# A hybrid attention and Hyena layer on one core: input loads placed further ahead of the casts that read them

## The chip, the cores and the metric

The kernel runs on one core of a Trainium2 chip. The metric is the device time of one execution in microseconds (us). PE is TensorE, DVE is VectorE, ACT is ScalarE, POOL is GpSimd, and SP is SyncE, which issues nearly all DMAs from one queue.

## The reference

One layer of an encoder over 2048 tokens of width 1024. One projection makes all inputs of two branches: windowed attention with a bias by relative position, and a long convolution (Hyena) whose filter is computed by a small network.

```
u = x @ w_in
q, k, v, a_gate, hy, h_gate, br_gate = split(u)
y_a = windowed_gqa(q, k, v, rel_bias, sink) * silu(a_gate)   # |i-j| <= 128, blocks of 128 queries
x0, x1, hv = split(short_conv(hy, conv_w, conv_b))           # width 3
h = sin(freq * (z @ w1 + b1)); h = sin(freq * (h @ w2 + b2)); h = sin(freq * (h @ w3 + b3))
h_f, h_b = decay * (h @ w4)                                  # the long filter, two sides
z = hv * x1
z = irfft(rfft(z) * rfft(filter)) + z * skip
y_h = z * x0 * silu(h_gate)
merged = g_a * (y_a @ w_branch_attn) + g_h * (y_h @ w_branch_hyena)
out = layer_norm(2 ** 0.25 * x + merged @ w_out)
```

There are 16 query heads and 4 heads of keys and values, each of width 64. All is fp32.

## The kernel before

**Numbers in two parts.** Each fp32 matmul operand is split into a high half (a cast to fp32r, `...h`) and a low half (the difference, `...l`), and a product is three matmuls: high by high, high by low, low by high. A split is thus a cast, mostly on ACT, and a subtraction on POOL or DVE, which waits for the cast. Names in the profile are those of tiles: `qh`, `ql`, `w4h`, `w4l`, `xq` (both halves of an input of a transform), `xS1h` and so on.

**Stages**, in order of the span: a projection stage for the first half of the channels (`hy_stage(0)`, to 375 us); the filter network (`filter_mlp`, L534) beside projections of keys, values and gates (to about 515); the filter's output, in units called quads (to 670); attention over the first eight heads (`attention(0)`, to about 1000, with projection work between its blocks); the second projection stage (1070 to 1380); the transform of the filter (to 1480); attention over the other heads (to 1850); 64 forward transforms of the convolution (`fwd`, L917, to 2150) with the attention branch's projection (`attn_out`, L1033) as filler; the inverse transforms; the merge and the output projection (2310 to the end).

**Order.** Each engine runs its instructions in an order that a scheduler decided when the kernel was built. The matmuls made with `mmo` keep the order of the program, and `tc.issue_after(x)` keeps what is under it behind `x`. So an instruction that waits holds back all that is behind it on its engine.

**Attention.** The work comes in groups: a pair of heads and two or three blocks of 128 queries. `groups` for the first half are of 3, 2 and 2 blocks, 24 groups with 56 blocks in all; for the second half they are of 3, with 72 blocks. At each step the loop (L826 to L846) issues the QK products of one block (`st_qk`, L720; PSUM `ps_a`), the transposes of the block before (`st_tr`; `ps_b`, then `ph` and `pl`) and the PV products of the one before that (`st_pv`; `ps_c`), with units of projection work between (`take`). `setup(i)` (L678) issues the loads of group i: bias, the q rows into `ql` (two buffers), the gate rows into `ag` (one buffer). `q_split(i)` (L700) casts `ql` to `qh` on ACT (L706) and subtracts on POOL in place (L707). It is placed behind the last exponential that the step issued:

```
                    if n == gctx[i]["b0"]:
                        setup(i + 1)
                    elif n == gctx[i]["b0"] + 1:
                        q_split(i + 1, last_exp[0])
```

`b0` and `b1` are the first and last block of group i, and n is the block of this step.

**Transforms.** `fwd_in(n)` (L907) loads the input of transform n, casts it on ACT (L911) and subtracts on POOL in two halves (L913). `x_half` gives it buffers, from a ring of 12 that the projection's operands used before. `enter_fft` calls it for the first `PRE` = 2 transforms at the end of attention 1, and `fft_next(n)` calls it for n + PRE after `fwd(n)`. `fwd` copies a product to `ka` on ACT (L927) and then runs six DVE operations (L931 to L936, and the split at L939). In the same time `load_big` (L115) brings `w_branch_attn` through the stage `ws` into the tiles `xA11`, `xA12`, `xS2` and `xS1`, with the subtraction on POOL.

**Filter.** `filter_mlp` computes the three sine layers in four parts of 512 columns: steps on DVE in tiles `sy` and `sk` (L553 to L561), the sine on ACT (L567). `filter_setup` (L584) then loads the last weights, `filt_w4`, in two parts into the ring of `sy` (L593 to L594) and splits them, the low half on DVE.

Of the kernel before, what the change touches and what calls it, by code (L numbers as in the profile page):

```python
# [8 lines left out]
F32 = mybir.dt.float32  # L9
# [5 lines left out]
P = 128  # L15
# [11 lines left out]
W_RING = 5  # L27
PRE = 2
LAST = (0.98, 0.99)
# [18 lines left out]
def hybrid_layer_kernel(ctx: ExitStack, tc: tile.TileContext, a: dict, out: bass.AP):  # L48
# [81 lines left out]
    with p1:  # L130
# [4 lines left out]
        zedge = const.tile([P, KT], F32, name="zedge")  # L135
        cw = const.tile([P, 24, 4], F32, name="cw")

        def consts():
            nc.sync.dma_start(out=cw, in_=a["conv"])
            nc.sync.dma_start(out=ident, in_=a["ident"])  # L140
            nc.sync.dma_start(out=sink, in_=a["attn_sink"].partition_broadcast(P))
# [201 lines left out]
        def hy_stage(p):  # L343
            base = 1024 * p
            with pool(f"hy{p}") as hy:
                hyp[0] = hy

                def raw(i):
# [107 lines left out]
                if p == 0:  # L456
# [10 lines left out]
                    for k in range(4):  # L467
                        r1.append(raw(4) if k % 2 == 0 else
                                  w_raw().rearrange("p a c -> p (a c)").rearrange("p (a c) -> p a c", a=2))
                        load_x(0, 1, k, r1[k])  # L470
                    consts()
                    for k in range(4):
# [61 lines left out]
        def filter_mlp(fl):  # L534
            Hv = h_d.rearrange("p a b -> p (a b)")
            fv = fl.tile([P, 4], F32, name="fv")
            nc.sync.dma_start(out=fv, in_=a["filt_vec"])
            w1 = fl.tile([66, P], F32, name="w1")
            w2 = fl.tile([P, P], F32, name="w2")
# [4 lines left out]
            for c in range(NCH):  # L544
# [3 lines left out]
                for l, w in enumerate((w1, w2, w3)):  # L548
# [14 lines left out]
                    if l < 2:  # L563
                        cur = fl.tile([P, CH], F32, name="sh", bufs=2)
                    else:
                        cur = fl.tile([P, CH], F32, name="H", bufs=2)
                    nc.scalar.activation(out=cur, in_=y, func=AF.Sin)  # L567
# [13 lines left out]
            for h in range(NH):  # L581
                nc.sync.dma_start(out=rep_d[h], in_=vec_d[h:h + 1].partition_broadcast(P))

        def filter_setup(fl, wr):  # L584
            dl = fl.tile([P, D], F32, name="dl")
# [5 lines left out]
            for g in range(2):  # L591
                gs = slice(g * CH, (g + 1) * CH)
                w4r = wr.tile([P, CH], F32, name="sy", bufs=2)  # L593
                nc.sync.dma_start(out=w4r, in_=a["filt_w4"][:, gs])  # L594
                split(w4h[:, gs], w4l[:, gs], w4r)
            s1k = fl.tile([P, 2, P], F32R, name="s1k")
# [46 lines left out]
        def attention(p, at, last=None):  # L643
# [34 lines left out]
            def setup(i):  # L678
# [6 lines left out]
                if g == 0:  # L685
                    if qt % 2 == 0:
                        load_kv(qt // 2)
                    for h in range(2):
                        bias[2 * qt + h] = at.tile([P, 384], F32, name="bias", bufs=3)
                        nc.sync.dma_start(out=bias[2 * qt + h], in_=skew(rep_d, 2 * qt + h))  # L690
                qh = at.tile([P, 2, 384], F32R, name="qh", bufs=2)
                ql = at.tile([P, 2, 384], F32R, name="ql", bufs=2)
                qv = q_d[qt, :, tok].rearrange("(h p) w -> p h w", h=2).bitcast(F32)
                for r in range(2):
                    nc.sync.dma_start(out=ql[r * 64:r * 64 + 64, :, 0:W].bitcast(F32), in_=qv)
                ag = at.tile([P, 384], F32, name="ag")
                nc.sync.dma_start(out=ag[:, 0:W], in_=ag_d[qt, :, tok])
                gctx[i] = dict(qt=qt, g=g, b0=b0, b1=b1, ag=ag, tok=tok, W=W, q=(qh, ql))

            def q_split(i, after=None):  # L700
# [122 lines left out]
            take(84 + 48)  # L823
            q_split(0)
            f0 = taken[0]
            for s in range(NS + 2):  # L826
                def part(x):
                    take(f0 + (total - f0) * min((s + PARTS[p][x]) / NS, 1.0))
                if s < NS:
                    st_qk(s)  # L830
                    i, n = steps[s]
                    if n == gctx[i]["b0"]:
                        setup(i + 1)
                    elif n == gctx[i]["b0"] + 1:
                        q_split(i + 1, last_exp[0])
                part(0)
                if s == NS and last:
# [13 lines left out]
        with pool("fc") as fc:  # L851
            with pool("ml") as ml:
                filter_mlp(ml)
                cs = filter_setup(fc, ml)
                run(stream([k_unit(ml, 0), v_unit(ml, 0)] + ag_units(ml, 0), mm))
# [50 lines left out]

        def fwd_in(n):  # L907
            f, g = divmod(n, 2)
            h, l = x_half(), x_half()
            last_ld[:] = [nc.sync.dma_start(out=l.bitcast(F32), in_=zk_d[:, f, g].bitcast(F32))]  # L910
            nc.scalar.copy(out=h, in_=l.bitcast(F32))  # L911
# [5 lines left out]
        def fwd(n, hl):  # L917
# [8 lines left out]
            k = fa.tile([P, CH], F32, name="ka", bufs=2)  # L926
            nc.scalar.copy(out=k, in_=kp)  # L927
            t1 = bank("t")
# [27 lines left out]
        wa, wg = [], []  # L956
        ins, ys = {}, {}

        def enter_fft(i):
            nonlocal fa  # L960
            if i == 0:
# [3 lines left out]
                for n in range(PRE):  # L965
                    fwd_in(n)
                wg[:] = [load_big("w_branch_attn", (nc.gpsimd, nc.gpsimd),
# [6 lines left out]
        def fft_next(n):  # L974
            f = n // 2
            if n + PRE < 64:
                fwd_in(n + PRE)
            if n % 2 and f + 1 < 32:
# [373 lines left out]
```

## Time and profile before

| what | us |
|---|---|
| median of three runs | 2743.44 |
| lowest and highest | 2738.68, 2751.53 |
| the profiled execution | 2745.46 |
| its span, from the first to the last instruction | 2743.7 |
| PE busy | 2547.3 (93%) |
| DVE, ACT, POOL busy | 1733.4, 1503.1, 1406.5 |

The profile is of one execution. Its mean granted clock of TensorE is 0.972 of full speed. Busy time of PE includes matmuls that run at the lower clock, so the time lost is found in two places: where PE is idle, and where the granted clock is below 1.00. A wait is put down to the instruction that ended it.

### The profile page before, as it was taken

The page shows a single profiled execution, that of the slowest core. Times are in us where ns is not written, and L with a number is a line of the kernel's source. Part 1 is how long each engine was busy: PE and PEld are TensorE (multiplying, and loading weights), DVE is VectorE, ACT ScalarE, POOL GpSimd, SP SyncE. Part 2 cuts the span into 40 slices and gives each one's busy share as a digit, 9 for nine tenths or more (in the row PEclk, how much of TensorE's full clock was granted, in tenths as well). Part 3 has the DMA queues.
Part 4 walks back from the last instruction along what each step waited for, and adds up shares of the span by engine and source line. Part 5 has one row for each costly group of instructions (what it writes and reads, how often), then busy time and mean ns, then how long its engine had stood idle before and what let it go on. Part 6 is the DMA issues. An engine that isn't in the chain of part 4 may idle for free.

```text
span 2743.7 us, 40487 instructions
## 1 busy us (share of the span) xinstructions
PE 2547.3 (93%) x13132; PEld 2143.8 (78%) x13132; DVE 1733.4 (63%) x3330; ACT 1503.1 (55%) x2897; POOL 1406.5 (51%) x1403
## 2 busy tenths in 40 slices
PE   6999999899998899999999999995999877999998
PEld 4888877686777777888877888884888766888887
DVE  8766677456666685665531777777899422555554
ACT  4444444477777674445555887886666443332231
POOL 6655545474656555655546666669666442211110
PEclk8999999999999999999999999998999998999999
DMA  5633443545444453346577444538787566644442
GB/s 199 213 123 115 133 134 124 164 154 203 124 124 132 132 173 121 100 129 201 176 242 237 133 137 141 154 111 283 236 256 236 201 217 216 204 154 154 150 139 81
DMA packets 275690, 456.54 MB, mean 166 GB/s; under 512 B 33513, under 2 KB 147515, under 8 KB 273925
## 3 DMA queue, kind: packets, MB, share of 16 engines
q1 hardware_dynamic: 273861, 444.90, 51.0%
q0 software_dynamic: 1616, 9.04, 1.0%
q8 instruction: 104, 1.70, 0.3%
q14 instruction: 109, 0.89, 0.1%
HBM read 294.42 MB, written 172.27 MB: 170 GB/s over the span
## 4 chain that ended last, share of the span: by engine, by line
PE 48%; DMA 9%; DVE 8%; POOL 3%; issue 3%; ACT 2%; SPq 0%; POOLq 0%; DVEq 0%; ACTq 0%
PE ps_y L53 8%; PE ps_a L53 4%; PE ps_c L53 4%; PE ps_y L271 4%; PE ps_y L273 4%; PE ps_y L275 4%; PE ps_zz L53 3%; PE ps_b L53 3%; PE ps_b L99 3%; DMA ga<-br_d 2%; DMA fl<-gc_d 2%; PE ps_zz L271 1%; PE ps_zz L275 1%; PE ps_zz L273 1%; DVE yl L57 1%
## 5 line engine op out<-in xcount | busy, mean ns | idle before, releaser
L57 POOL TENSOR_TENSOR w_l<-w_tmp,w_h 128x512 fp32r<-128x512 f32 x272 | 374.2, 1377 | 315.9 <-ACT w_h L56 277.7
L57 POOL TENSOR_TENSOR w_l<-w_raw,w_h 128x512 fp32r<-128x512 f32 x204 | 300.5, 1474 | 159.4 <-ACT w_h L56 131.5
L56 ACT CAST w_h<-w_tmp 128x512 fp32r<-128x512 f32 x272 | 168.2, 620 | 227.8 <-PE ps_y L273 174.1
L1157 POOL TENSOR_TENSOR ar<-ar,ga 128x256 f32<-128x256 f32 x64 | 48.3, 757 | 316.3 <-ACT ga L1156 177.1
L56 ACT CAST w_h<-w_raw 128x512 fp32r<-128x512 f32 x204 | 126.5, 621 | 152.3 <-PE ps_zz L273 88.6
L755 ACT ACTIVATE pb<-pb,rm 128x385 f32<-128x385 f32 (+1 forms) x256 | 153.2, 600 | 89.5 <-DVE rm L752 80.2
L913 POOL TENSOR_TENSOR xq<-xq 128x512 fp32r<-128x512 f32 x128 | 162.3, 1291 | 71.1 <-ACT xq L911 56.2
L370 DVE SCALAR_TENSOR_TENSOR cv<-u,cw,cv 128x1024 f32<-128x1024 f32 (+1 forms) x96 | 138.8, 1447 | 68.3 <-ACT cv L367 68.1
L271 PE MATMUL ps_y<-xq,w_h 128*128 128x512 f32 x376 | 152.1, 404 | 5.4 <-ACT u L283 5.2
L273 PE MATMUL ps_y<-xq,w_h 128*128 128x512 f32 x376 | 148.4, 395 | 0.0
L275 PE MATMUL ps_y<-xq,w_l 128*128 128x512 f32 x376 | 148.1, 394 | 0.0
L749 DVE CUSTOM_DVE_ANT_0 pb<-ps_a,bias 128x384 f32<-128x384 f32 (+1 forms) x256 | 130.1, 534 | 26.5 <-PE ps_a L53 22.5
L57 DVE TENSOR_TENSOR pl<-ps_b,ph 128x512 fp32r<-128x512 f32 (+1 forms) x240 | 128.5, 560 | 22.6 <-ACT ph L56 20.9
L224 DVE TENSOR_TENSOR w_tmp<-w_raw 128x512 f32<-128x512 f32 x94 | 97.1, 1033 | 57.8 <-DMA w_raw<-in_w_in_dram 40.3
L224 DVE TENSOR_TENSOR w_tmp<-w_raw,w_tmp 128x512 f32<-128x512 f32 x94 | 90.9, 967 | 63.5 <-POOL w_l L57 62.7
L283 ACT COPY u<-ps_y 128x512 f32<-128x512 f32 x204 | 118.8, 582 | 8.7 <-PE ps_y L275 8.0
L53 PE MATMUL ps_y<-xq,w_h 128*128 128x512 f32 x336 | 113.1, 406 | 1.2 <-ACT u L283 1.2
L56 ACT CAST ph<-ps_b 128x512 fp32r<-128x512 f32 (+1 forms) x240 | 106.7, 485 | 12.7 <-PE ps_b L99 10.5
L53 PE MATMUL ps_a<-k,ql 128*128 128x384 f32 (+1 forms) x256 | 86.7, 341 | 26.6 <-POOL ql L707 26.6
L287 DVE TENSOR_TENSOR ev<-ps_zz,u 128x512 f32<-128x512 f32 x72 | 49.4, 686 | 87.5 <-ACT u L283 41.2
L1000 PE MATMUL ps_y<-yh,b 128*128 128x256 f32 x344 | 99.7, 292 | 4.8 <-DVE ga L1158 4.7
L53 PE MATMUL ps_c<-pl,v 128*128 128x256 f32 x368 | 98.7, 294 | 5.5 <-DVE pl L57 5.1
(406 smaller groups left out, 8746.4 us busy)
## 6 DMA issues: line engine op xcount, KB each, us to landing
w_raw<-in_w_in_dram SPq DMA_DIRECT2D x136, 512.0 KB
xq<-zk_d SPq DMA_DIRECT2D x64, 512.0 KB
br_d<-ev SPq DMA_DIRECT2D x64, 256.0 KB
zk_d<-ko SPq DMA_DIRECT2D x64, 256.0 KB
zk_d<-zo SPq DMA_DIRECT2D x64, 256.0 KB
gc_d<-go SPq DMA_DIRECT2D x64, 256.0 KB
fl<-gc_d SPq DMA_DIRECT2D x32, 512.0 KB
ga<-br_d SPq DMA_DIRECT2D x64, 256.0 KB
```

The lines of the kernel that those rows point to most:

```text
L53: tc.keep_in_program_order(nc.tensor.matmul(*args, **kw))
L56: nc.scalar.copy(out=hi, in_=src)
L57: return (eng or nc.vector).tensor_tensor(out=lo, in0=src, in1=hi.bitcast(F32), op=ALU.subtract)
L224: w_sum[0].tensor_tensor(out=self.tmp[n], in0=i0, in1=i1, op=ALU.subtract)
L271: mmf(o, wh[:, k], xh[k], start=start and k == 0, stop=False, skip_group_check=not start)
L273: mmf(o, wh[:, k], xl[k], start=False, stop=False, skip_group_check=not start)
L275: mmf(o, wl[:, k], xh[k], start=False, stop=k == 3, skip_group_check=not start)
L283: nc.scalar.copy(out=u.tmp[n], in_=o)
L370: nc.vector.scalar_tensor_tensor(out=y[:, i0:hi], in0=u[:, i0 + n:hi + n], scalar=cw[:, t, n:n + 1], in1=y[:, i0:hi], op0=ALU.mult, op1=AL ...
L749: nc.vector.tensor_tensor_reduce(out=pb[:, 0:W], in0=sc[:, 0:W], in1=bias[head][:, off:off + W], scale=1.0, scalar=-3.0e38, op0=ALU.add, o ...
L755: last_exp[0] = nc.scalar.activation(out=pb[:, 0:W + 1], in_=pb[:, 0:W + 1], func=AF.Exp, bias=rm[:, 1:2], accum_out=rm[:, 2:3])
L913: nc.gpsimd.tensor_tensor(out=l[:, i], in0=l[:, i].bitcast(F32), in1=h[:, i].bitcast(F32), op=ALU.subtract)
```

## The change

Three places are changed, and one tile moves.

- In attention 0, the q rows of group i + 2 are loaded at the last block of group i (`q_load`), into a ring of three buffers, and `q_split(i + 1)` stands at the first block of group i, not the second. In attention 1 (p = 1) the split stays at the second block.
- In the transforms, a load and a split are now apart: the load is four transforms ahead (`PRE`), the split two ahead and behind the copy `ka` of the current transform.
- `filt_w4` is loaded into two tiles of its own ahead of the network's other weights, and its low half is subtracted on POOL. `H` has one buffer, not two.
- `cw`, the weights of the short convolution, is a tile of each projection stage, not of the whole program, and is loaded at the start of each.

```diff
-PRE = 2
+PRE = 4
...
-        cw = const.tile([P, 24, 4], F32, name="cw")
+        cw = None
...
             with pool(f"hy{p}") as hy:
                 hyp[0] = hy
+                cw = hy.tile([P, 24, 4], F32, name="cw")
+                if p == 1:
+                    nc.sync.dma_start(out=cw, in_=a["conv"])
...
             nc.sync.dma_start(out=fv, in_=a["filt_vec"])
+            w4 = []
+            for g in range(2):
+                w4.append(fl.tile([P, CH], F32, name="w4", bufs=2))
+                nc.sync.dma_start(out=w4[g], in_=a["filt_w4"][:, g * CH:(g + 1) * CH])
...
-                        cur = fl.tile([P, CH], F32, name="H", bufs=2)
+                        cur = fl.tile([P, CH], F32, name="H", bufs=1)
...
-                w4r = wr.tile([P, CH], F32, name="sy", bufs=2)
-                nc.sync.dma_start(out=w4r, in_=a["filt_w4"][:, gs])
-                split(w4h[:, gs], w4l[:, gs], w4r)
+                split(w4h[:, gs], w4l[:, gs], w4[g], nc.gpsimd)
...
+                if i not in qls:
+                    q_load(i)
                 qh = at.tile([P, 2, 384], F32R, name="qh", bufs=2)
-                ql = at.tile([P, 2, 384], F32R, name="ql", bufs=2)
-                qv = q_d[qt, :, tok].rearrange("(h p) w -> p h w", h=2).bitcast(F32)
-                for r in range(2):
-                    nc.sync.dma_start(out=ql[r * 64:r * 64 + 64, :, 0:W].bitcast(F32), in_=qv)
+                ql = qls.pop(i)
...
+            def q_load(i):
+                if i >= len(seq):
+                    return
+                qt, g = seq[i]
+                b0, b1 = groups[g]
+                W = (b1 - b0 + 1) * P
+                qls[i] = at.tile([P, 2, 384], F32R, name="ql", bufs=3 - p)
+                qv = q_d[qt, :, b0 * P:b0 * P + W].rearrange("(h p) w -> p h w", h=2).bitcast(F32)
+                for r in range(2):
+                    nc.sync.dma_start(out=qls[i][r * 64:r * 64 + 64, :, 0:W].bitcast(F32), in_=qv)
...
             q_split(0)
+            if p == 0:
+                q_load(1)
...
                         setup(i + 1)
-                    elif n == gctx[i]["b0"] + 1:
+                    if n == gctx[i]["b0"] + p:
                         q_split(i + 1, last_exp[0])
+                    if p == 0 and n == gctx[i]["b1"]:
+                        q_load(i + 2)
...
-        def fwd_in(n):
+        def fwd_load(n):
             f, g = divmod(n, 2)
-            h, l = x_half(), x_half()
-            last_ld[:] = [nc.sync.dma_start(out=l.bitcast(F32), in_=zk_d[:, f, g].bitcast(F32))]
+            raws[n] = x_half()
+            last_ld[:] = [nc.sync.dma_start(out=raws[n].bitcast(F32), in_=zk_d[:, f, g].bitcast(F32))]
+
+        def fwd_split(n):
+            l, h = raws.pop(n), x_half()
             nc.scalar.copy(out=h, in_=l.bitcast(F32))
...
-            nc.scalar.copy(out=k, in_=kp)
+            last_k[:] = [nc.scalar.copy(out=k, in_=kp)]
...
                 for n in range(PRE):
-                    fwd_in(n)
+                    fwd_load(n)
+                for n in range(2):
+                    fwd_split(n)
...
             if n + PRE < 64:
-                fwd_in(n + PRE)
+                fwd_load(n + PRE)
+            if n + 2 < 64:
+                with tc.issue_after(last_k[0].ins):
+                    fwd_split(n + 2)
```

The change shifts line numbers by up to some 30: the cast of q is L706 before and L725 after, its subtraction L707 and L726, the exponential L755 and L774; the subtraction of a transform's input is L913 and L938.

On ACT, in attention 0, at a group of two blocks, before the change (`L755` exponentials, `L763` the scaling of the second head, `ph` the cast of transposed probabilities, `w_h` filler):

```order
L763 ACTIVATE pb<-pb,rm 128x384
L755 ACTIVATE pb,rm<-pb,rm 128x385 x2
L56 CAST w_h<-w_tmp 128x512
L56 CAST ph_6454<-ps_b 128x512
L56 CAST ph_6461<-ps_b 128x256
L763 ACTIVATE pb<-pb,rm 128x384
L755 ACTIVATE pb,rm<-pb,rm 128x385 x2
L706 CAST qh<-ql 128x768
```

And after it, at the same place:

```order
L782 ACTIVATE pb<-pb,rm 128x384
L56 CAST w_h<-w_tmp 128x512
L774 ACTIVATE pb,rm<-pb,rm 128x385 x2
L725 CAST qh<-ql 128x768
L56 CAST ph_6456<-ps_b 128x512
L56 CAST ph_6463<-ps_b 128x256
L782 ACTIVATE pb<-pb,rm 128x384
L56 CAST w_h<-w_raw 128x512
L774 ACTIVATE pb,rm<-pb,rm 128x385 x2
```

The cast of the next group's q (128x768) stands behind the exponentials of the group's first block, and no longer behind those of its second.

On POOL, at the start of the transforms, before the change (`xS2l` and `xS1l` are low halves of `w_branch_attn`, `xq` those of transform inputs, two instructions for one input):

```order
L57 TENSOR_TENSOR xS2l<-ws,xS2h 128x512
L913 TENSOR_TENSOR xq<-xq 128x512 x4
L57 TENSOR_TENSOR xS1l<-ws,xS1h 128x512
L913 TENSOR_TENSOR xq<-xq 128x512 x2
L57 TENSOR_TENSOR xS1l<-ws,xS1h 128x512
L913 TENSOR_TENSOR xq<-xq 128x512 x2
L57 TENSOR_TENSOR xS1l<-ws,xS1h 128x512
L913 TENSOR_TENSOR xq<-xq 128x512 x2
L57 TENSOR_TENSOR xS1l<-ws,xS1h 128x512
L913 TENSOR_TENSOR xq<-xq 128x512 x20
```

And after it:

```order
L57 TENSOR_TENSOR xS2l<-ws,xS2h 128x512
L57 TENSOR_TENSOR xS1l<-ws,xS1h 128x512
L938 TENSOR_TENSOR xq<-xq 128x512 x2
L57 TENSOR_TENSOR xS1l<-ws,xS1h 128x512
L938 TENSOR_TENSOR xq<-xq 128x512 x2
L57 TENSOR_TENSOR xS1l<-ws,xS1h 128x512 x2
L938 TENSOR_TENSOR xq<-xq 128x512 x24
L57 TENSOR_TENSOR ayl<-ayl,ayh 128x512
```

Between the last `xS2l` and the last `xS1l` stand ten subtractions of transform inputs before the change and four after it. Counted from the start of the transforms, 36 stand ahead of the last `xS1l` before and 26 after.

On DVE, at the end of the filter network, before the change (`ev` ends a projection unit and frees its PSUM bank):

```order
L224 TENSOR_TENSOR w_tmp<-w_raw,w_tmp 128x512
L287 TENSOR_TENSOR ev<-ps_zz,u_4074 128x512
L57 TENSOR_TENSOR w4l<-sy,w4h 128x512
L224 TENSOR_TENSOR w_tmp<-w_raw 128x512
L57 TENSOR_TENSOR w4l<-sy,w4h 128x512
L287 TENSOR_TENSOR ev<-ps_y_4355,u_4343 128x512
L287 TENSOR_TENSOR ev<-ps_zz,u_4730 128x512
```

And after it:

```order
L223 TENSOR_TENSOR w_tmp<-w_raw,w_tmp 128x512
L286 TENSOR_TENSOR ev<-ps_zz,u_4074 128x512
L223 TENSOR_TENSOR w_tmp<-w_raw 128x512
L286 TENSOR_TENSOR ev<-ps_y_4355,u_4343 128x512
L286 TENSOR_TENSOR ev<-ps_zz,u_4730 128x512
```

The two subtractions `w4l` have left DVE, where they stood ahead of two `ev`; on POOL they stand near the start of the network.

## Rows read from the trace of the kernel before

**Rows 1.** Windows by stage: busy us of each engine, clock, DMA share, GB/s.

```profile
375.00:515.00 140.00, 127.87 (x542) 99.42 (x540) 96.57 (x141) 60.51 (x110) 64.06 (x46) 0.99 0.44 147
...
670.00:1045.00 375.00, 335.51 (x1751) 285.44 (x1751) 250.61 (x750) 256.97 (x595) 215.64 (x264) 0.95 0.47 145
...
1850.00:2150.00 300.00, 259.12 (x1463) 220.92 (x1462) 268.25 (x403) 194.62 (x320) 206.87 (x165) 0.95 0.74 243
```

**Rows 2.** Waits of PE, 670 to 1045: total us, times, longest.

```profile
PE ps_a L53 <- POOL ql L707: 25.1, 14, 3.9
PE ps_a L53 <- ACT qh L706: 5.1, 5, 3.1
```

**Rows 3.** Waits of PE in attention 1, 1475 to 1855.

```profile
PE ps_a L53 <- POOL ql L707: 1.4, 1, 1.4
```

**Rows 4.** Timeline of ACT, POOL and PE around one wait: start, duration.

```profile
756.69 0.60 ACT L755 ACTIVATE pb<-pb,rm 128x385 f32<-128x385 f32 x1
...
757.29 0.82 ACT L706 CAST qh<-ql 128x768 fp32r<-128x768 f32 x1
...
758.19 1.81 POOL L707 TENSOR_TENSOR ql<-ql,qh 128x768 fp32r<-128x768 f32 x1 [0.59 <-ACT qh L706]
...
760.05 0.39 PE L53 MATMUL ps_a<-k,ql 128*128 128x256 f32 x1 [1.29 <-POOL ql L707]
```

**Rows 5.** Windows of 20 us in attention 0.

```profile
700.00:720.00 20.00, 16.66 (x83) 14.28 (x82) 12.02 (x42) 11.69 (x28) 11.31 (x17) 0.83 0.35 103
...
940.00:960.00 20.00, 13.39 (x70) 11.32 (x69) 12.58 (x38) 12.98 (x30) 9.62 (x10) 0.83 0.39 130
...
980.00:1000.00 20.00, 16.82 (x81) 13.86 (x80) 19.30 (x38) 15.18 (x35) 14.34 (x14) 0.91 0.58 199
```

**Rows 6.** Windows: first to last QK of attention 0, and attention 1.

```profile
686.50:998.00 311.50, 274.40 (x1470) 235.60 (x1469) 217.55 (x694) 222.75 (x530) 186.30 (x242) 0.95 0.44 136
1497.00:1850.00 353.00, 347.08 (x1958) 304.14 (x1959) 270.85 (x895) 282.90 (x671) 234.51 (x301) 1.00 0.44 135
```

**Rows 7.** Timeline of SP's DMA issues in attention 0.

```profile
750.06 0.32 SPq L697 DMA_DIRECT2D ag<-ag_d  x1
...
756.08 1.24 SPq L695 DMA_DIRECT2D ql<-q_d  x2
```

**Rows 8.** Windows of 20 us in the transforms.

```profile
1870.00:1890.00 20.00, 12.29 (x42) 8.12 (x42) 19.33 (x30) 16.79 (x29) 20.00 (x17) 0.91 0.98 332
...
1910.00:1930.00 20.00, 10.29 (x47) 8.49 (x48) 10.19 (x16) 9.08 (x15) 16.11 (x14) 0.66 0.45 150
```

**Rows 9.** Waits of PE in the transforms, 1855 to 2155.

```profile
PE ps_b L53 <- POOL xS1l L57: 5.8, 2, 3.3
PE ps_b L53 <- ACT xS1h L56: 5.3, 2, 3.7
```

**Rows 10.** Groups of instructions, 1855 to 2155: count, busy us, mean ns.

```profile
L913 POOL TENSOR_TENSOR xq<-xq 128x512 fp32r<-128x512 f32 x122 | 154.6, 1291 | 68.3 <-ACT xq L911 56.2 <-PE ps_y L53 8.7 <-PE ps_c L53 1.9
```

**Rows 11.** Timelines of PE, DVE, ACT and SP at the filter network's end.

```profile
515.20 0.79 PE L271 MATMUL ps_y<-xA11h,w_h 128*128 128x512 f32 x1 [7.49 <-DVE ev L287]
...
519.06 0.40 PE L271 MATMUL ps_y<-xA11h,w_h 128*128 128x512 f32 x1
...
513.85 0.69 DVE L57 TENSOR_TENSOR w4l<-sy,w4h 128x512 fp32r<-128x512 f32 x1 [15.03 <-ACT w4h L56]
...
513.20 0.62 ACT L56 CAST w4h<-sy 128x512 fp32r<-128x512 f32 x1 [8.56 <-DMA sy<-in_filt_w_dram]
...
506.09 0.43 SPq L594 DMA_DIRECT2D sy<-in_filt_w_dram  x1
...
510.80 0.82 SPq L609 DMA_DIRECT2D hs<-h_d  x1
```

**Rows 12.** Matmuls that read `w4l`: ns min/median/max, first and last start.

```profile
L621 PE MATMUL ps_a<-w4l,hh x43: 387/393/398, 522.7 to 662.7; 128*128 128x512 f32 x43
```

**Rows 13.** A step of the network on DVE, in the same columns.

```profile
L559 DVE SCALAR_TENSOR_TENSOR sy<-sk,sy x36: 674/691/1791, 378.2 to 492.7; 128x512 f32<-128x512 f32 x36
```

More of the change, by code (lines that the diff above doesn't have):

```diff
@@ L135, in hybrid_layer_kernel @@
         zedge = const.tile([P, KT], F32, name="zedge")
-        cw = const.tile([P, 24, 4], F32, name="cw")
+        cw = None
         def consts():
-            nc.sync.dma_start(out=cw, in_=a["conv"])
             nc.sync.dma_start(out=ident, in_=a["ident"])
@@ L344, in hy_stage @@
             base = 1024 * p
+            nonlocal cw
             with pool(f"hy{p}") as hy:
                 hyp[0] = hy
+                cw = hy.tile([P, 24, 4], F32, name="cw")
+                if p == 1:
+                    nc.sync.dma_start(out=cw, in_=a["conv"])
                 def raw(i):
@@ L470, in hy_stage @@
                         load_x(0, 1, k, r1[k])
+                    nc.sync.dma_start(out=cw, in_=a["conv"])
                     consts()
@@ L582, in filter_mlp, with filter_setup @@
                 nc.sync.dma_start(out=rep_d[h], in_=vec_d[h:h + 1].partition_broadcast(P))
-        def filter_setup(fl, wr):
+            return w4
+        def filter_setup(fl, w4):
             dl = fl.tile([P, D], F32, name="dl")
@@ L698, in setup @@
                 gctx[i] = dict(qt=qt, g=g, b0=b0, b1=b1, ag=ag, tok=tok, W=W, q=(qh, ql))
+            qls = {}
+            def q_load(i):
[8 more added lines that the diff above has]
+                    nc.sync.dma_start(out=qls[i][r * 64:r * 64 + 64, :, 0:W].bitcast(F32), in_=qv)
             def q_split(i, after=None):
@@ L852, in hybrid_layer_kernel @@
             with pool("ml") as ml:
-                filter_mlp(ml)
-                cs = filter_setup(fc, ml)
+                cs = filter_setup(fc, filter_mlp(ml))
                 run(stream([k_unit(ml, 0), v_unit(ml, 0)] + ag_units(ml, 0), mm))
@@ L956, in hybrid_layer_kernel @@
         wa, wg = [], []
-        ins, ys = {}, {}
+        ins, ys, raws, last_k = {}, {}, {}, []
         def enter_fft(i):
```

## The prediction

> **What bounds the kernel now.** I read the windows by stage first. TensorE (PE) is busy 93% of the span, so time can only come out of its idle stretches and out of stretches at the lower clock. The first attention stage (670 to 1045) has 39.5 us without PE work and a mean granted clock of 0.95; the forward transforms (1850 to 2150) have 40.9 us and 0.95; the stretch of the filter network (375 to 515) has 12.1 us [rows 1]. The change touches these three.
>
> In the first, the waits of PE name one cause: `ps_a` (the QK product) waits 25.1 us in 14 places for POOL's q low half and 5.1 us in 5 places for ACT's q high half, together 30.2 us [rows 2]. In attention 1, which has the same functions, the first of these waits is 1.4 us, once [rows 3]. The timeline of one such wait shows why: ACT runs the second exponential of a block at 756.69, then the q cast at 757.29 (0.82 us), POOL subtracts at 758.19 for 1.81 us, and the next group's QK, already queued, starts at 760.05 after 1.29 us of waiting [rows 4]. The cast stands behind the exponentials of the group's second block, and in a group of two blocks the very next block belongs to the next group. Attention 1 has groups of three blocks and so one block more to spare.
>
> The waits cost the clock as well. Of the 20-us windows of this stage, four (from 700, 780, 900 and 940) show a granted clock of 0.83, a mixture of the two levels, 2.4 and 1.2 GHz; the first and the last of them stand in [rows 5]. The waits are in just those stretches.
>
> In the transforms DVE is the bound: busy 268.25 of 300 us [rows 1] and 19.33 of 20 us in a full window, but only 10.19 us in 1910 to 1930, where PE falls to 10.29 us and the clock to 0.66 [rows 8]. There `ps_b` waits 5.8 us for POOL's and 5.3 us for ACT's half of `xS1`, the last tiles of `w_branch_attn` [rows 9]. POOL, which had no idle time in the window at 1870 [rows 8], works in program order through subtractions for the transforms (122 of 1.29 us [rows 10]) and those of `xS1`.
>
> **Attention 0: the split one block earlier, the load one group earlier.** No instruction is added. Cast and subtraction move ahead by one block. A block of this stage takes 311.5 us / 56 = 5.6 us now [rows 6]. The longest wait for the low half is 3.9 us [rows 2], under one block, so in the usual case all are covered. I leave the 1.4 us that attention 1 still has: 30.2 − 1.4 = 28.8 us. For the clock, four windows lose 20 × 0.17 = 3.4 us each, 13.6 us at most; PE was idle in part of that time (3.34 of 20 us in the first, 6.61 in the last [rows 5]), and what fell into idle time cost nothing, so I take three quarters, 10 us. What is late next: ACT is busy 222.75 and DVE 217.55 of 311.5 us [rows 6]. If the stage shrinks to 273 us these are 82% and 80%; attention 1 runs at 80% and 77% (282.90 and 270.85 of 353) with clock 1.00 [rows 6], so the ordinary blocks can do it, but the end cannot shrink: in 980 to 1000 DVE is busy 19.30 us with x operands for the next stage [rows 5]. I give back 3 us. **Term: −36 us.** The ceiling comes from attention 1's rate: 353 us / 1958 matmuls = 0.180 us, times 1470 is 265 us, 46 us less than now [rows 6]. The floor is three quarters of the waits and nothing of the clock, −22 us.
>
> The load has to be there for the earlier cast. SP issues in order, and in the row of interest it sits on the gate load `ag` until 750.06 and then on the q load, which waits for the QK that reads its buffer, until 756.08 [rows 7]. With a third buffer that second wait is gone, and the new place of the q load is right behind that `ag` load, some 6 us sooner, against a cast some 5.6 us sooner. So the lead stays what it is, and it is enough now.
>
> **Transforms: loads four ahead, splits two ahead.** The casts, subtractions and loads are as many as before. ACT, which sat on late inputs, gets them earlier. By the order, 26 subtractions of transform inputs stand ahead of the last `xS1` subtraction where 36 did: 10 × 1.29 = 12.9 us of POOL less [rows 10]. But the new splits wait for the current transform's copy `ka`, so POOL will idle for perhaps half of that. I let 6 of the 11.1 us of waiting [rows 9] go, and 1 us for the half clock there. **Term: −7 us**; the ceiling is both waits, −11 us, since DVE at 19.33 of 20 us leaves nothing elsewhere. Against it: two more input loads before the first transform. The window at 1870 moves 332 GB/s at a DMA share of 0.98 [rows 8], so 2 × 0.5 MB delay the matrices and weights behind them by up to 3.2 us; the bound is +3 us.
>
> **Filter network.** The second `filt_w4` load is issued at 506.09, behind the stores of `rep_d`; ACT waits 8.56 us for it until 513.20; DVE's subtraction follows at 513.85; the `ev` of a finished unit is queued behind that on DVE, and its PSUM bank holds PE for 7.49 us until 515.20. The nine matmul starts from there to 519.06 are 0.43 us apart, the pace of the lower level [rows 11]; at the upper one they would take half, 1.9 us less. With `w4` loaded 130 us earlier, 7.5 + 1.9 = 9.4 us come free. Late next is `hs`, issued at 510.80 [rows 11]: the first matmul of the filter's output stood at 522.7 [rows 12] and would come to 513.3, where `hs` has hardly landed and still needs a cast. I give back 2.9 us for that and a clock that dips anyway. **Term: −6.5 us**, bounds −2 and −9.4.
>
> POOL's two subtractions of `w4` come near 380, off any wait. Some DVE steps of the network's chain take up to 1791 ns there, against a median of 691 [rows 13], so by that row two more overlaps cost 2 × 1.1 = 2.2 us. The chain is hidden behind projection matmuls until its end; if `hs` is what is late next, the term is −4.3. The Trainium skill, SBUF — State Buffer, section "Who interferes with whom", speaks against moving work to POOL: a DVE instruction with two SBUF inputs and a GpSimd one that reads SBUF exclude each other, and whoever issues first keeps the other out for its whole length. By that rule the same two steps would wait up to 1.3 us each; the trace agrees in kind, with the 1791 ns.
>
> **The rest.** `w4` first means two issues of 0.43 us [rows 11] ahead of the network's small weights: 0 to 0.9 us, taken as 0, because projections fill PE then. The convolution weights are loaded a second time before the second projection stage, one small load where SP has room: 0, bound 7 us (from the issue at 506.09 to the landing at 513.20, a queued load [rows 11]).
>
> **Sum.** −36 − 7 − 6.5 = −49.5 us. The profiled execution took 2745.46 us around a span of 2743.7; it becomes 2696. That execution is 2.0 us above the median of 2743.44, so the median becomes **2694 us**. The three runs before lie 0.47% apart; 0.5%, 13.7 us, is about what can be told from no change.
>
> **Rivals.** (1) *Only part of the waits returns, because ACT takes the cast ahead of the softmax of the second block.* The cast of 0.82 us [rows 4] now stands before that block's reads of `ph` and its exponentials, and ACT at 82% has little slack; then `ps_c` waits where `ps_a` did. For it: the chain of one block runs through ACT several times. Against it: attention 1 carries the cast between blocks as well, and waits little. Attention −22, transforms −3, filter −4: −29, giving 2714 us.
>
> (2) *The change does not do what it says in attention 0*, because q loads come late: SP is stuck on `ag` [rows 7] beyond the cast and ACT stops for the landing. Only the other two terms, −13.5, are left: 2730 us. Against it: the lead worked out above.
>
> (3) *Slower, in the transforms.* The split of input n+2 is issued after the copy `ka` of transform n, together with `ayl` subtractions on the same engine. If POOL's half comes after the PE wants it by one subtraction (1.29 us [rows 10]) in each of 62 transforms, that is +80 us against −42.5 elsewhere: 2781 us. It turns the sign from 0.7 us each on. Against it: POOL is busy 206.87 of 300 us [rows 1], and a transform lasts over 4 us, so the low half has about two of them.
>
> (4) *More*: all waits [rows 2, 9, 11] and the clock: −46 − 11 − 9 = −66, 2677 us.
>
> **Chances.** The forecast (2682 to 2706) 0.62; rival 1 0.22; rival 2 0.06; rival 3 0.04; rival 4 0.06. The range 2672 to 2722 holds the forecast, rival 4 and most of rival 1. Faster by over 0.5%: forecast, rivals 1 and 4 and half of rival 2, 0.93; within 0.5%: the other half, 0.03, and a small rival 3, 0.01; slower 0.03.
>
> **What would show it.** In the profile after: the wait of `ps_a` for `ql` and `qh` in attention 0 under 5 us, that stage's clock near 1.00 and its length near 336 us; ACT's wait for `w4h` gone and PE's 7.49 us down to 2 or less; PE's waits for `xS1` below 6 us. Rival 1 shows as `ps_c` waiting for `ph` or `pl`, rival 2 as ACT's cast waiting for a DMA, rival 3 as PE's `ps_a` waiting for `xq` from POOL in the transforms. What would make it wrong most: a new wait in attention 0 that keeps the clock at 0.83, since the clock and the waits of this stage are three quarters of the sum.

## The result and the profile after

The changed kernel takes 2703.25 us (median of 4, 2699.46 to 2711.21) against 2747.49 of the kernel before on the same chip: ratio 0.9835, 95% interval 0.9811 to 0.986, so 1.65% faster. The profiled execution took 2705.55 us, with a span of 2703.8 and a mean clock of 0.977. The forecast was 2694, range 2672 to 2722.

The total is near, but one of the three terms went the other way. I compare the two traces by the first and last start of what begins and ends a stage (us, from the start of the span; QK is the product of queries and keys, the first matmuls of an attention block):

| stretch | before | after | difference |
|---|---|---|---|
| start to the first QK of attention 0 | 686.5 | 697.9 | +11.4 |
| first to last QK of attention 0 | 311.7 | 277.9 | −33.8 |
| from there to the first QK of attention 1 | 497.5 | 501.1 | +3.6 |
| first to last QK of attention 1 | 354.1 | 349.5 | −4.6 |
| last QK to the last forward transform | 289.1 | 282.5 | −6.6 |
| from there to the end of the span | 604.8 | 594.9 | −9.9 |

**Attention 0** did what was forecast. These are the windows from the first to the last QK of both stages, in the columns of [rows 6]:

```profile
697.90:975.80 277.90, 265.10 (x1471) 230.38 (x1470) 213.46 (x690) 219.64 (x525) 187.13 (x242) 0.98 0.49 151
1477.00:1826.00 349.00, 343.82 (x1954) 302.10 (x1955) 267.99 (x894) 282.70 (x671) 232.66 (x298) 1.00 0.45 137
```

Beside [rows 6], PE's idle time in attention 0 went from 37.1 us (311.50 − 274.40) to 12.8 (277.90 − 265.10), 24.3 less, and the busy time of the same 1470 matmuls from 274.4 to 265.1, 9.3 less, since fewer of them run at the lower clock (0.95 to 0.98). The list of PE's waits, 690 to 1010, names no `ql` and no `qh` any more; what is late next is small (the first of these two waits was 2.0 us before):

```profile
PE ps_c L53 <- DVE pl L57: 6.6, 11, 1.2
PE ps_c L53 <- ACT pb L774: 5.0, 1, 5.0
```

The lower clock is left at the stage's end alone. The 20-us windows have 1.00 up to 920, then 0.83, 0.91 and 0.91; the first of the slow ones, which holds the wait of 5.0 us for `pb`, is

```profile
920.00:940.00 20.00, 14.95 (x70) 12.57 (x69) 13.47 (x36) 13.34 (x32) 12.10 (x14) 0.83 0.43 139
```

**Transforms.** PE's waits from 1826 to 2126, to be read beside [rows 9]:

```profile
PE ps_a L53 <- POOL xq L938: 8.3, 5, 4.5
...
PE ps_c L53 <- DMA mat<-s_d: 5.0, 1, 5.0
...
PE ps_b L53 <- POOL xS1l L57: 1.8, 1, 1.8
```

The waits for `xS1` fell from 11.1 us to 1.8. In their place stand 8.3 us for inputs that POOL has not yet subtracted. The 5.0 us for the first matrix only look new: the kernel before waits nearly as long at the same matmul, the first of the transforms, where the wait is put down to DVE's `ya`. The timelines of PE show it, first before, then after:

```profile
1861.76 1.62 PE L53 MATMUL ps_c<-xq,mat 128*128 128x512 f32 x3 [4.59 <-DVE ya L812]
```

```profile
1837.15 1.62 PE L53 MATMUL ps_c<-xq,mat 128*128 128x512 f32 x3 [5.01 <-DMA mat<-s_d]
```

It starts 12.0 us behind the last QK before and 10.8 us after.

**Filter.** The stretch that [rows 1] shows with 12.1 us of idle PE has 8.8 now, but its clock fell from 0.99 to 0.96, and the quads behind it have 9.1 us idle, against 3.1 (155.00 − 151.94) in the same window before:

```profile
375.00:515.00 140.00, 131.24 (x534) 100.90 (x533) 104.00 (x141) 60.11 (x110) 59.85 (x46) 0.96 0.40 132
515.00:670.00 155.00, 145.91 (x592) 112.08 (x592) 98.27 (x129) 105.46 (x185) 91.41 (x77) 0.97 0.44 152
```

The wait of 7.49 us [rows 11] is gone. In its place, in the timelines of ACT and PE, stand an early one for `filt_w4` and a late one for the network's output:

```profile
370.36 0.62 ACT L56 CAST w4h<-w 128x512 fp32r<-128x512 f32 x1 [3.80 <-DMA w<-in_filt_w_dram]
...
524.08 0.80 PE L627 MATMUL ps_a<-w4h,hh 128*128 128x512 f32 x1 [3.64 <-ACT hh L56]
```

### The profile page after: what moved, and what is told of

Its sections match the earlier page's. It is cut to its first block, busy times and chain, and to the rows that moved or that the text cites. A ratio compares the mean times of both kernels' runs of the same rounds, so it can differ in the third digit from the quotient of the medians.

```text
span 2703.8 us, 40522 instructions
## 1 busy us (share of the span) xinstructions
PE 2535.4 (94%) x13132; PEld 2136.0 (79%) x13132; DVE 1738.7 (64%) x3328; ACT 1500.6 (56%) x2897; POOL 1414.5 (52%) x1405
## 4 chain that ended last, share of the span: by engine, by line
PE 63%; DVE 13%; DMA 13%; issue 4%; ACT 4%; POOL 3%; SPq 1%; DVEq 0%; POOLq 0%; ACTq 0%
PE ps_y L53 9%; PE ps_y L270 7%; PE ps_y L272 6%; PE ps_y L274 6%; PE ps_a L53 4%; PE ps_c L53 4%; PE ps_zz L53 3%; PE ps_b L99 3%; PE ps_b L53 3%; DMA ga<-br_d 3%; PE ps_zz L270 3%; PE ps_zz L272 3%; PE ps_zz L274 3%; DMA fl<-gc_d 2%; DVE yl L57 1%
## 5 line engine op out<-in xcount | busy, mean ns | idle before, releaser
L938 POOL TENSOR_TENSOR xq<-xq 128x512 fp32r<-128x512 f32 x128 | 162.6, 1295 | 60.5 <-ACT xq L936 58.9
L774 ACT ACTIVATE pb<-pb,rm 128x385 f32<-128x385 f32 (+1 forms) x256 | 153.2, 600 | 72.2 <-DVE rm L771 61.5
L57 DVE TENSOR_TENSOR pl<-ps_b,ph 128x512 fp32r<-128x512 f32 (+1 forms) x240 | 130.1, 560 | 12.8 <-ACT ph L56 11.2
L99 PE MATMUL ps_b<-ident,pb 128*128 128x128 f32 x736 | 102.6, 275 | 0.0
```

The costliest lines, as they stand in the source:

```text
L57: return (eng or nc.vector).tensor_tensor(out=lo, in0=src, in1=hi.bitcast(F32), op=ALU.subtract)
L99: return nc.tensor.transpose(out=o, in_=i, identity=ident)
L774: last_exp[0] = nc.scalar.activation(out=pb[:, 0:W + 1], in_=pb[:, 0:W + 1], func=AF.Exp, bias=rm[:, 1:2], accum_out=rm[:, 2:3])
L938: nc.gpsimd.tensor_tensor(out=l[:, i], in0=l[:, i].bitcast(F32), in1=h[:, i].bitcast(F32), op=ALU.subtract)
```

## The experiments

Twelve kernels ran, four at a time on one chip, each four beside runs of the kernel before (medians 2746.01, 2751.88 and 2750.38 us). So ratios to the kernel before are compared, not times; the bracket behind a ratio is its 95% interval. The first four take the change apart.

**e1_no_filter**: the changed kernel without its filter part.

```diff
-            w4 = []
-            for g in range(2):
-                w4.append(fl.tile([P, CH], F32, name="w4", bufs=2))
-                nc.sync.dma_start(out=w4[g], in_=a["filt_w4"][:, g * CH:(g + 1) * CH])
...
-                split(w4h[:, gs], w4l[:, gs], w4[g], nc.gpsimd)
+                w4r = wr.tile([P, CH], F32, name="sy", bufs=2)
+                nc.sync.dma_start(out=w4r, in_=a["filt_w4"][:, gs])
+                split(w4h[:, gs], w4l[:, gs], w4r)
```

> The changed kernel without its filter part: filt_w4 comes through the ring of sy at the end again and is split on DVE. Theory A (the filter part costs time: in the profile after, the first QK of attention 0 starts 11.4 us later than before): about 2703 - 11 = 2692 us, and the first QK back at about 686 us. Theory B (as predicted, the filter part gains 6.5 us, and the late start has another cause, such as the conv weights' tile or a difference between executions): about 2703 + 6.5 = 2710 us, and the first QK stays near 698 us.

Measured: 0.9822 (0.979 to 0.9854), 2694.51 us; the first QK at 687.7. Theory A by the trace; the ratio alone does not part it from the whole change.

**e2_q_only**, **e3_fft_only** and **e4_filter_only**: the kernel before with the lines of one part of the diff each (with the first, `cw` moves too).

```diff
-                    elif n == gctx[i]["b0"] + 1:
+                    if n == gctx[i]["b0"] + p:
```

> The kernel before with the attention part alone (q split a block earlier, q load a group earlier, three buffers, and the conv weights in the projection stages, which make the room). Theory A (the stage's 33.8 us from the first to the last QK are this part's): 34 us less than before, about 2713 us, with the first to the last QK of attention 0 in 278 us. Theory B (a third or more of the stage's gain comes from what the filter part puts ahead of it, work that now runs before the first QK): no more than 23 us less, about 2724 us, with that stretch at 288 us or more.

Measured: 0.9854 (0.9833 to 0.9874), −40 us of 2746; first to last QK 274.1 us. Theory A.

```diff
-PRE = 2
+PRE = 4
...
+                with tc.issue_after(last_k[0].ins):
+                    fwd_split(n + 2)
```

> The kernel before with the transforms' part alone. Theory A (6.6 us, as between the two profiles from the last QK to the last transform): about 2740 us. Theory B (the inverse and merge stages, 9 us shorter in the profile after, owe this to the transforms' part too): 15 us less, about 2732 us. Theory C (nothing, what xS1 gives is lost to the matrix load and the POOL waits): 2747 us.

Measured: 0.9958 (0.9943 to 0.9972), −12 us; last QK to last transform 284.7 us. Between A and B: the stage itself gave 4.4 us, and the rest is not in one place.

```diff
-                split(w4h[:, gs], w4l[:, gs], w4r)
+                split(w4h[:, gs], w4l[:, gs], w4[g], nc.gpsimd)
```

> The kernel before with the filter part alone. Theory A: 11 us more than before, about 2758 us, slower by 0.4%, with the end of the network's chain some 8 us later. Theory B: 6.5 us less, about 2741 us.

Measured: 1.0044 (1.0028 to 1.006), +12 us. Theory A: the filter part alone makes the kernel slower. The chain of the network ended at 503.0 us, against 494.7 before.

The next two divide the filter part.

**e5_filter_late**: loads behind the first features, split behind the last sine.

```diff
-                split(w4h[:, gs], w4l[:, gs], w4[g], nc.gpsimd)
+                with tc.issue_after(last_sin[0].ins):
+                    split(w4h[:, gs], w4l[:, gs], w4[g], nc.gpsimd)
```

> The changed kernel with filt_w4 still in tiles of its own, but loaded behind the network's small weights and first features, and cast and subtracted behind the network's last sine. Theory A (the filter part loses by its early cast: ACT waits 3.8 us for the load at 370 us with the work of a projection unit behind it, and the network's chain slides 8.6 us; the order of the quads costs the rest): the chain ends near 497 us, the first quad comes at 515 to 519, the first QK at about 691 instead of 698 us, in all about 2696 us. Theory B (the early cast is harmless, the whole loss is the order in which the quads are run): first QK at 697 us, 2703 us.

Measured: 0.9861 (0.9837 to 0.9884); chain's end 503.3, first QK 705.3. Theory A fell: without the early cast the chain was as late, and PE waited 5.3 us more, for an `ev` on ACT just ahead of the first QK. Nor is it B alone, since the chain still ended late.

**e6_own_tiles_only**: as e1, but `filt_w4` in tiles of its own (and `H` with one buffer).

```diff
-                w4r = wr.tile([P, CH], F32, name="sy", bufs=2)
+                w4r = wr.tile([P, CH], F32, name="w4", bufs=2)
```

> The changed kernel without its filter part, except that filt_w4 has tiles of its own instead of the ring (and H one buffer): loads and splits stand in the program where they stood before, behind the stores of the bias rows. The order of the quads on PE then is that of the changed kernel. Theory A (the order of the quads at their end costs 6 to 9 us by itself): from the first quad to the first QK 170 us or more, against 163 us without the filter part; first QK at 694 us or later, about 2700 us. Theory B (the order of the quads costs nothing): 163 us for that stretch, first QK at 688 us or earlier, about 2693 us.

Measured: 0.9807 (0.9784 to 0.983). Without the ring to wait for, SP issued the loads at 371.93 although they stand late in the program, and ACT waited 6.3 us for the first of them, but the chain ended at 496.9 and the first quad came at 517.5, 7.1 us sooner than in e1. From there to the first QK it took 173.5 us against 163.1. Theory A by that stretch, though the first QK, at 691.0, came sooner than it said (694).

Two divide the attention part.

**e7_q_split_only** and **e8_q_load_only**, both from e2:

```diff
-            if p == 0:
-                q_load(1)
...
-                    if p == 0 and n == gctx[i]["b1"]:
-                        q_load(i + 2)
```

> Attention part alone, with the cast a block earlier and three buffers, but the load issued by setup, one group ahead as before. Theory A (the earlier load is needed): ACT's cast waits for its DMA in most groups, 1 us or more each; the stretch from the first to the last QK is 285 us or more instead of 274, in all about 2716 us. Theory B (a third buffer lets SP issue the load early enough from its old place): 274 us and 2704 us, as with the whole attention part.

Measured: 0.9834 (0.9812 to 0.9856); first to last QK 274.8 us. Theory B: with a third buffer the old place of the load does as well.

```diff
-                    if n == gctx[i]["b0"] + p:
+                    if n == gctx[i]["b0"] + 1:
```

> Attention part alone, with the load two groups ahead into three buffers, but the cast at its old place in the group's second block. Theory A (the place of the cast is the cause): PE still waits some 30 us for q, the stretch stays at 311 us, about 2746 us. Theory B (the loads were late): 275 us and 2706 us.

Measured: 1.0001 (0.9982 to 1.0019); 311.6 us. Theory A. PE's waits, 680 to 1010, stay those of [rows 2]:

```profile
PE ps_a L53 <- POOL ql L723: 26.1, 14, 4.3
PE ps_a L53 <- ACT qh L722: 5.6, 6, 3.2
```

**e9_h_ring**: the whole change with another filter part. `filt_w4` goes into the two buffers of `H`, loaded ahead of the stores of `rep_d`, split on DVE.

```diff
+            for g in range(2):
+                w4.append(fl.tile([P, CH], F32, name="H", bufs=2))
+                nc.sync.dma_start(out=w4[g], in_=a["filt_w4"][:, g * CH:(g + 1) * CH])
             nc.sync.dma_start(out=vec_d, in_=vec)
```

> The changed kernel with another filter part: filt_w4 goes into the two buffers of H, loaded in the program ahead of the stores of the bias rows (SP then issues the second load behind 8 of the 16 stores), split on DVE. The quads keep the order of the kernel before. Theory A (the loss is the sliding chain plus the order of the quads, and the wait for filt_w4 was worth 7 us): chain's end near 497 us, first quad at 517 to 520, first QK at 681 to 684 us, in all 2687 to 2690 us, better than without the filter part (2694). Theory B (hs and the rest of SP's queue hold the first quad anyway): first quad at 523 us or later, first QK at 687 us, 2694 us.

Measured: 0.9809 (0.9788 to 0.9831), 2695.52 us; first quad 519.2, first QK 683.6. Theory A by the trace, though the total is 5 us above what it said. Its interval overlaps those of the change, of e1 and of e6, so the ratio does not make it the best of them.

**e10_filter_dve**: the whole change, the low half of `filt_w4` on DVE.

```diff
-                split(w4h[:, gs], w4l[:, gs], w4[g], nc.gpsimd)
+                split(w4h[:, gs], w4l[:, gs], w4[g])
```

> The changed kernel with the low half of filt_w4 subtracted on DVE, as before the change, loads and tiles as in the change. Theory A (POOL's two subtractions at 371 us hold a weight's low half, DVE waits 3.1 us for it and the chain slides): the chain ends near 497 us, first QK at 691 us, about 2697 us. Theory B (where it is subtracted does not matter; the load ahead of the small weights, ACT's wait for it or the order does): chain's end at 503 us, first QK at 697 us, about 2703 us.

Measured: 0.9857 (0.9836 to 0.9878); chain's end 502.9, first QK 705.4. Theory A fell. The chain ended as theory B said, but the first QK came 8 us later than it said; 4.7 us of this is the wait for an `ev` on ACT that e5 has as well.

**e11_fft_no_pace** and **e12_fft_pre2**: the whole change, splits not behind `ka`, and loads two ahead.

```diff
-                with tc.issue_after(last_k[0].ins):
-                    fwd_split(n + 2)
+                fwd_split(n + 2)
```

> The changed kernel with the splits of the transforms' inputs two ahead, but not held behind the copy ka; loads four ahead. Measured from the last QK of attention 1 to the last transform: 282.5 us with the whole part, 287 to 290 us without it. Theory A (holding the splits back is what lets the last tiles of w_branch_attn through): 288 us, about 2709 us, with PE's waits for xS1 back near 11 us. Theory B (the loads four ahead are what counts): 282 us, 2703 us.

Measured: 0.9893 (0.9869 to 0.9918), last QK to last transform 289.6 us. Theory A. PE's waits, 1819 to 2119, show `xS1` again:

```profile
PE ps_b L53 <- ACT xS1h L56: 9.3, 2, 5.2
...
PE ps_c L53 <- DMA mat<-s_d: 5.3, 1, 5.3
...
PE ps_b L53 <- POOL xS1l L57: 2.2, 2, 1.6
```

```diff
-PRE = 4
+PRE = 2
```

> The changed kernel with the transforms' inputs loaded two ahead (PRE = 2), splits behind ka. Theory A (the order of the splits counts): 282 us from the last QK to the last transform, or a little less, since the matrices are no longer behind four loads (the wait of 5.0 us for mat gone): 278 us, about 2699 us. Theory B (the loads count): ACT waits for its inputs again as before, 288 us or more, 2709 us.

Measured: 0.9851 (0.9827 to 0.9876), 284.4 us. Nearer to A; the wait for `mat` stayed (5.1 us), so the four loads are not its cause.

All stretches in us, from the traces (the chain's end is the start of the network's last sine, the first quad the first matmul that reads `w4h`; "DVE `tl`" is DVE's busy time on `tl` from 515 to 710; the last two columns run from the first to the last QK of attention 0, and from the last QK of attention 1 to the last forward transform):

| kernel | chain's end | first quad | to first QK | DVE `tl` | QK of attention 0 | transforms |
|---|---|---|---|---|---|---|
| before | 494.7 | 522.5 | 164.0 | 24.8 | 311.7 | 289.1 |
| after | 503.3 | 524.1 | 173.8 | 33.8 | 277.9 | 282.5 |
| e1_no_filter | 497.3 | 524.6 | 163.1 | 25.3 | 275.3 | 282.5 |
| e2_q_only | 497.1 | 524.1 | 164.8 | 25.0 | 274.1 | 287.4 |
| e3_fft_only | 497.2 | 523.3 | 164.0 | 25.0 | 311.9 | 284.7 |
| e4_filter_only | 503.0 | 523.0 | 173.1 | 32.6 | 314.3 | 290.2 |
| e5_filter_late | 503.3 | 524.8 | 180.5 | 34.1 | 275.6 | 283.3 |
| e6_own_tiles_only | 496.9 | 517.5 | 173.5 | 35.2 | 274.0 | 282.8 |
| e7_q_split_only | 497.9 | 525.9 | 164.6 | 24.5 | 274.8 | 285.7 |
| e8_q_load_only | 497.4 | 524.6 | 164.1 | 25.2 | 311.6 | 290.1 |
| e9_h_ring | 496.6 | 519.2 | 164.4 | 24.5 | 277.0 | 282.8 |
| e10_filter_dve | 502.9 | 523.4 | 182.0 | 35.2 | 275.1 | 280.0 |
| e11_fft_no_pace | 499.2 | 519.6 | 172.7 | 34.3 | 276.7 | 289.6 |
| e12_fft_pre2 | 497.8 | 518.2 | 173.9 | 32.8 | 274.3 | 284.4 |

## Why the prediction was right, and where not

**Attention 0, −36 us: right, in mechanism and size.** The four executions with the cast at its old place have 311.6 to 314.3 us between the first and last QK, the ten with the earlier cast 274.0 to 277.9: 37 us between the means (312.4 and 275.5). e8 and e7 show that the place of the cast is all of it (both have the third buffer; the earlier cast with two buffers was not run). The load two groups ahead gives nothing by itself and is not needed for the rest; that the lead of the load was enough already was argued from [rows 7], and holds. The give-back came as rival 1 describes it (waits of `ps_c` for `pl` and for an exponential, 11.6 us), but stayed small. The clock gave 9.3 us where 10 were forecast, though one reading behind that was off: not all the waits are in the four slow windows, but 18.0 of the 30.2 us, and two more windows (from 860 and 980) stood at 0.91.

**Transforms, −7 us: right in size, in mechanism only in part.** Means of the table's last column: 288.5 us for the five kernels without this part (before, e2, e4, e7, e8), 282.7 for the seven with all of it, 5.8 us. The cause was as stated, the splits being held behind `ka`, which lets `xS1` through (e11). But that is not where the balance comes from: the waits for `xS1` fell by 9.3 us, and waits for `xq` from POOL of the same size came (8.3 us of `ps_a` and 1.0 of `ps_c`). This is what rival 3 describes, in 6 places and not in each of 62 transforms. What is left of the gain stands in PE's waits for DVE's `t`, 15.6 us before and 8.9 after, for which the sum had no term; so that the size came out is partly luck. The bound against it, matrices delayed by the loads, did not show: the first matrix is waited for 5 us with two early loads as with four (e12) and also without the pace (e11), and the kernel before loses 4.6 us at the same place.

**Filter, −6.5 us: wrong, and the sign with it.** That the wait for `filt_w4` held PE was right, and so was "Late next is `hs`" (3.64 us for `hh` above). Up to the first quad the term is worth what was said: in e6 the first quad comes 7.1 us sooner than in e1. The step that failed is that all else was left as it stood: the stretch of the quads behind that matmul has no term, and the chain was taken to stay hidden "until its end". e9, which keeps the old order of the quads, does bring 4.1 us to the first QK (683.6 against 687.7 in e1); of the gain of the change nothing reached it, for two reasons.

The first is the stretch of the quads. In all seven kernels in which `filt_w4` has tiles of its own it takes 172.7 us or more to the first QK, in the seven others 163.1 to 164.8; the medians (173.8 and 164.1) are 9.7 us apart. (The two longest, e5 and e10, hold the wait for an `ev` on ACT besides.) The scheduler puts the quads' matmuls in another order there: the fourteen traces have just two orders, one in each seven. Here is a piece of PE's order without projection work, Q for a matmul of `w4` and s for one of `s1k`, with the number in a row, before and after:

```
before: s4 Q3 s2 Q3 s4 Q3 s6 Q4 s2 Q2 s1 Q3 s3 Q3 s2 Q3 s4
after:  Q3 s1 Q3 s5 Q3 s3 Q3 s1 Q3 s5 Q3 s3 Q3 s1 Q3 s5
```

The seven with tiles of its own also have one buffer for `H`, the others two. That is not the cause: the order can be read from a kernel that is built and not run, and e1 built with one buffer for `H` keeps the old order, e6 built with two the new one. Why the scheduler reorders is open; e5, where `filt_w4` is cast only at 503.9, has the new order too.

With the new order the splits of the quads shift against each other. Of the two halves of a pair, DVE subtracts one low half `tl` and POOL the other. The groups of DVE's instructions, 615 to 660, show what one costs, first before, then after, then in e6 and e9:

```profile
L57 DVE TENSOR_TENSOR tl<-dc,th 128x512 fp32r<-128x512 f32 x14 | 9.6, 686 | 3.9 <-ACT th L56 3.9
```

```profile
L57 DVE TENSOR_TENSOR tl<-dc,th 128x512 fp32r<-128x512 f32 x12 | 13.2, 1120 | 1.1 <-ACT th L56 0.8
```

```profile
L57 DVE TENSOR_TENSOR tl<-dc,th 128x512 fp32r<-128x512 f32 x12 | 15.8, 1343 | 1.2 <-ACT th L56 1.0
```

```profile
L57 DVE TENSOR_TENSOR tl<-dc,th 128x512 fp32r<-128x512 f32 x15 | 10.3, 688 | 3.7 <-ACT th L56 3.7
```

The same instruction, 686 ns before and 1120 to 1343 in the new order. The timelines of DVE and POOL after show it at one place:

```profile
646.08 1.30 POOL L57 TENSOR_TENSOR tl<-dc,th 128x512 fp32r<-128x512 f32 x1 [3.60 <-ACT th L56]
...
646.86 1.07 DVE L57 TENSOR_TENSOR tl<-dc,th 128x512 fp32r<-128x512 f32 x1
```

POOL's subtraction runs from 646.08 to 647.38; DVE's, started at 646.86, ends at 647.93, 0.55 us behind POOL's end, though alone it takes 0.69 us from its start: it was held up until POOL was done. This is no single case. Of the 448 `tl` of DVE in the fourteen traces, 162 take over 0.8 us, 6 in each kernel with the old order and 16 to 18 in each with the new one. Every one of the 162 started while a `TENSOR_TENSOR` ran on POOL and ends 0.54 to 0.56 us behind its end. The other way round, a `TENSOR_TENSOR` of POOL that starts while a `tl` runs on DVE ends 1.1 to 1.2 us behind that (195 cases). DVE's copies and products from PSUM, in the same groups, keep their 680 to 690 ns.

Over the whole stretch `tl` keeps DVE busy for 24.5 to 25.3 us in the old order and 32.6 to 35.2 in the new one, some 9 us more. The stretch is longer by about as much, but the one is not the measure of the other. PE's windows from the first quad to the first QK, before, then after:

```profile
522.50:686.50 164.00, 160.85 (x672) 123.20 (x671) 98.59 (x145) 115.42 (x202) 95.11 (x84) 1.00 0.48 164
```

```profile
524.10:697.90 173.80, 165.93 (x671) 126.93 (x672) 108.57 (x145) 117.53 (x205) 102.55 (x88) 0.97 0.46 159
```

Of the 9.8 us, 4.7 are idle time of PE (3.15 and 7.87) and 5.1 the longer busy time of the same 671 matmuls, at a mean clock of 0.97 against 1.00. Much of the second part stands right behind the wait for `hh`. In its first 7 us PE has no idle time in either kernel:

```profile
522.50:529.50 7.00, 7.00 (x32) 5.76 (x31) 6.11 (x9) 1.77 (x4) 1.49 (x2) 1.00 0.19 68
```

```profile
524.10:531.10 7.00, 7.00 (x18) 5.57 (x19) 3.41 (x4) 1.93 (x4) 4.66 (x5) 0.56 0.57 173
```

Before the change the clock was low ahead of the first quad instead (0.75 from 515.2 to 522.5, behind the wait of 7.49 us). The prediction let these 1.9 us come free; the low clock moved behind the first quad.

The rule that the prediction weighed at the two subtractions of `w4`, the Trainium skill, SBUF — State Buffer, section "Who interferes with whom", describes just this: a DVE instruction with two inputs in SBUF and a GpSimd one that reads SBUF exclude each other, and the first to issue keeps the other out to its end. The trace agrees, with 0.55 us behind POOL's end; it was weighed at 2 instructions, while 32 pairs stood elsewhere. The collisions are thus shown. That they, and not the order of PE in itself, cost PE the idle time is argued, from fourteen traces in which the two go together; in e6 5.1 of the 7.8 us of idle time are waits for DVE's `tl` and `dc`, before the change 0.6 of 3.1, but after it 2.2 of 7.9. A kernel with all `tl` on one engine, which would part them, was not run.

The second reason is the network's chain. It ended at 502.9 to 503.3 us in four of the six kernels that load `filt_w4` in `filter_mlp` into tiles of its own (after, e4, e5, e10), and at 494.7 to 499.2 in all others. "The chain is hidden behind projection matmuls until its end" was true, but not that it would stay where it was. What moves it is open: it stays late without the early cast (e5) and without POOL's subtraction (e10), while e11 and e12, with the filter part of the change unaltered, had it at 499.2 and 497.8, so that a part of it is the spread between executions. PE's wait for `hh` does not hang on it alone: it is 2.9 to 3.9 us in all seven kernels with tiles of its own. Four executions with that part have the first QK at 692.1 to 697.9, the six without any of it at 686.5 to 690.5, so its cost in a trace is 2 to 11 us, and 12 us by the ratio of e4.

**The sum** of −49.5 came out at −44.2 us (2703.25 − 2747.49). In the pair of profiles, −39.9 us of span, the three terms give −33.8 − 6.6 + 11.4 = −29.0. The other −10.9 lies in stretches that no term covers, mostly behind the transforms (−9.9), so the miss of the filter term was covered by what no term had; that the total came near the forecast is in part luck. I have no cause for it: that last stretch spreads from 594.9 to 604.8 us over the fourteen traces, and these two kernels have its two ends.

## What to carry to other kernels

When a wait for an input is taken away, ask also for the stretch behind it: a scheduler may reorder the work that uses an input when the input's tiles change, and the order of the changed kernel can be compared there before any run. Where VectorE and GpSimd share a split, look at the mean duration of one instruction of each, not at busy shares: the same form with two means hints at a collision, and the ends of the two instructions, a fixed time apart, show it. A cast in an in-order queue behind work of the wrong block can cost a wait in most groups (19 waits in 24 groups here), and moving it one block did here what an earlier load could not.

## What the runs showed of the hardware

A subtraction of 128x512 with both inputs in SBUF took VectorE 0.69 us alone and up to 1.78 us beside GpSimd's, so the same 32 instructions kept it busy for 25 or for 33 to 35 us in one stretch, by where they fell beside GpSimd's. And the lower clock cost in attention 0 a measurable 9.3 us of busy time over 1470 matmuls at a mean of 0.95 against 0.98.
